# Value projections of four head pairs merged into two, in a two-layer FoX and retention trunk

## The chip, the core and the metric

The kernel runs on one core of one Trainium2 chip. The metric is the device time of one execution in microseconds (us), median of several runs. The kernel before takes 941.47 us (three runs, 941.02 to 941.47). The engines are named as in the profile: PE (TensorE, matmuls), PEld (its weight loads), DVE (VectorE), ACT (ScalarE), POOL (GpSimd), SP (SyncE, which here only issues DMAs).

## The reference

Two decoder layers over 512 positions of width 1024. Each makes one big input projection, attends in 12 main heads of 128 (layer 0: attention with a forget gate; layer 1: retention) and in 4 heads over a memory of 256 positions, multiplies by a SiLU gate, and projects out to the residual stream.

```python
for i in range(DEPTH):                       # 2
    h = rmsnorm(x, norm_g[i])
    proj = h @ (fox_w_in if i == 0 else ret_w_in)
    q, k, v, (f_logit,) q_mem, z = split_cols(proj, ...)
    main = fox_attention(q, k, v, f_logit, fox_b_f) if i == 0 else retention(q, k, v)
    memo = mem_cross_attention(q_mem, mem_n, w_mem_kv[i])
    o = concatenate([main, memo]) * silu(z)
    x = x + o @ w_out[i]
return rmsnorm(x, final_norm_g)
# in retention, q and k (64 wide a head) are rotated first:
#   concatenate([t1 * cos - t2 * sin, t1 * sin + t2 * cos])
```

Everything is float32. The kernel writes each operand as a high part H and a low part L in the fp32r type and makes every product of three matmuls (H·H, H·L, L·H).

## The kernel before, in words

**Matmuls.** Activations h lie transposed as hH and hL, 8 slices of 128 rows (`k`) by 512 positions. Weights come in 148 pieces of 128x1024 (`load_piece`, SP's queue, 3 `raw` buffers); `prep_piece` turns each into wH (a cast on ACT, L130) and wL (a subtraction on DVE, L131). There are 4 buffers of wH and of wL. When a piece's last matmul is written, `retire` frees it and at once writes the preparation of the next piece in the order of use.

**Fillers.** The dense work is cut into fillers, pieces of some 2.8 us of PE time. `f_T` (matmuls at L220) makes a projection with the weights stationary and the 512 positions moving: 24 matmuls in two fillers of 12. Through it go the gate `f_z`, the queries and keys of layer 0 and of the memory `f_q`, and the rotated queries and keys of layer 1 `f_rot`. `f_v` makes the value projection of a pair of heads the other way round: the positions of a block `t` of 128 are stationary, 256 weight columns move, so that one filler is 24 matmuls of 256 columns (`mm_group`, L60), and a pair takes 4 fillers. `f_out` (also L60) makes the output projection, 12 matmuls of 512 columns a block.

**Attention steps.** Between the fillers stand the steps of the attention of the current pair (`g_fox`, `g_ret`). In `g_ret` a step is a score (two matmuls, L60, of k and the two parts of q, into a tile `s`), the product with the values (`o`, two steps of six matmuls), and a norm (matmul of ones).

**The order.** PE is in the order in which the program writes it (`MANUAL`); the other engines are ordered by a scheduler, by a priority that each step gets from its filler's number. `build_layer` writes one `cycle` a pair: a list of fillers and the attention steps, spread over the fillers by `mode`. In cycle `pr` the attention of pair `pr` runs, and the fillers make the values of `pr`, the gates z0 and z1 of `pr`, and the queries and keys `nq` of pair `pr + 1`. The first score of a pair is written right behind the first filler of its cycle (the fifth for pair 0 of layer 1).

**The rotation.** In `f_rot` the finished projection (tile `acc`) is copied by ACT into `r` (L243), four DMAs on SP's queue swap its quarters into `sw` (L246), DVE multiplies and adds (L248, L249, L250), ACT casts (L254, L260), and DVE subtracts: L256 for k, L261 for q. The DVE work has the priority of four fillers later (`PRIO[3]`). Only behind the L256 of a head may a score read that head's k. In layer 1 the kernel before writes `nq` of pairs 1 and 3 ahead of z0 and z1, and `nq` of pairs 2 and 4 between the halves of the output projection, so that four fillers of its cycle come after the rotated k:

```python
            elif pr in (2, 4):
                o = f_out(l, (pr - 2, pr - 1))
                f = f + z0 + z1 + o[:4] + nq + o[4:]
...
            elif l == 0:
                f = f + z0 + z1 + nq
            else:
                f = f + nq + z0 + z1
```

**Tiles.** `vv` (5 buffers of 4 KB a partition) holds the values, the memory's values (in layer 1 reloaded by POOL, L441) and some row tiles; PSUM has 3 `acc`, 2 `s` and 3 tiles for transposes and `o`.

Of the kernel before, what the change touches and what calls it, by code (L numbers as in the profile page):

```python
# [9 lines left out]
F32R = mybir.dt.float32r  # L10
# [9 lines left out]
EPS = 1e-6  # L20
NEG_SCALE = -1.0 / math.sqrt(128.0)
BIG = 1e30
BUFS = dict(raw=3, w=4, qk=10, sqs=2, vv=5, gg=8, sz=2, pT=1, dd=5, p=2, cbc=2, km=6, acc=3, s=2, at=3)
TAGS = dict(acc="acc", s="s", t="at", o="at")
MANUAL = ("PE",)
TLS = False
# [10 lines left out]
def tile_hybrid(ctx, tc, x_in, mem_in, memT_in, g_cols, norm_g, fin_g, b_f, wv0, wp, index, consts, cosT, sinT, dec, out):  # L37
    nc = tc.nc
    P = 128
    KD = D // P  # L40
    NT = S // P
# [9 lines left out]
    def ps_at(kind, shape, dt, name):  # L51
        tag = TAGS[kind]
        return psum.tile(shape, dt, name=name, tag=tag, bufs=BUFS[tag])

    V, A, G, PE = nc.vector, nc.scalar, nc.gpsimd, nc.tensor
# [6 lines left out]
    def split3(lh, ll, rh, rl):  # L62
        return [(lh, rh), (lh, rl), (ll, rh)]
# [11 lines left out]
    def tile_(tag, shape, dt=F32):  # L75
        return work.tile(shape, dt, name=tag, bufs=BUFS[tag])

# [9 lines left out]
    hH = xp.tile([P, KD, S], F32R, name="hH")  # L87
    hL = xp.tile([P, KD, S], F32R, name="hL")
# [3 lines left out]
    st = {}  # L92
# [11 lines left out]
    raws, pieces = {}, {}  # L104
# [31 lines left out]
    def retire(*keys):  # L136
        for k in keys:
            pieces.pop(k)
            with due(first_use.get(order[min(nprep[0], len(order) - 1)], 0) + PRIO[2]):
                prep_piece()  # L140
# [8 lines left out]
    def split_to(dH, dL, src, scale=None):  # L149
        if scale is None:  # L150
            A.copy(out=dH, in_=src)  # L151
            V.tensor_tensor(out=dL, in0=src, in1=dH.bitcast(F32), op=ALU.subtract)
        else:
            A.activation(dH, src, AF.Copy, scale=scale)
            V.scalar_tensor_tensor(out=dL, in0=src, scalar=scale, in1=dH.bitcast(F32), op0=ALU.mult, op1=ALU.subtract)
# [6 lines left out]
    def acc_tile():  # L162
        return ps_at("acc", [P, 512], F32, name="acc")
# [102 lines left out]
    def f_v(l, pr):  # L266
        keys = [(l, "v", pr, i) for i in range(2)]
        first = l == 0 and pr == 0
        n = 268 if first else 256
        per = 1 if first else 2  # L270
        box = {}

        def part(t):
            if t == 0:
                st[l, "v", pr] = [tile_("vv", [P, 4, 256], F32R) for _ in range(2)]
                if first:
                    st["fl"] = small.tile([P, NT, 12], F32, name="fl", bufs=1)
            vH, vL = st[l, "v", pr]
            if t % per == 0:
                box["ps"] = acc_tile()  # L280
            ps, u = box["ps"], t % per
            terms = []
            for i, key in enumerate(keys):
                H, L = pieces[key]
                for k4 in range(4):
                    k = i * 4 + k4
                    terms += split3(hH[:, k, t * P:(t + 1) * P], hL[:, k, t * P:(t + 1) * P],
                                    H[:, k4 * n:(k4 + 1) * n], L[:, k4 * n:(k4 + 1) * n])
            mm_group(ps[:, u * 256:u * 256 + n], terms)
            if u == per - 1:  # L290
                src = ps[:, :per * 256].rearrange("p (u c) -> p u c", u=per)
                split_to(vH[:, t + 1 - per:t + 1, :], vL[:, t + 1 - per:t + 1, :], src)
                if first:
                    V.tensor_tensor(out=st["fl"][:, t, :], in0=ps[:, 256:268], in1=bfb, op=ALU.add)
            if t == NT - 1:
                retire(*keys)
        return [(keys if t == 0 else [], lambda t=t: part(t)) for t in range(NT)]

    def out_terms(l, pc, heads, t, c0=0, c1=512):
        H, L = pc  # L300
# [16 lines left out]
    def f_out(l, pairs):  # L317
        heads = [h for pr in pairs for h in (pr * 2, pr * 2 + 1)]
        res = []
        for hf in range(2):  # L320
            keys = [(l, "o", pr, hf) for pr in pairs]
            step = 3 - len(pairs)
            for t in range(0, NT, step):
                def fn(t=t, hf=hf, keys=keys):
                    for t2 in range(t, t + step):
                        out_block(l, [pieces[k] for k in keys], heads, t2, hf)
                    if t + step == NT:
                        retire(*keys)
                res.append((keys if t == 0 else [], fn))
        return res  # L330
# [385 lines left out]
    def build_layer(l):  # L716
        M = "fox" if l == 0 else "ret"
        fq = (lambda pr: f_q(0, "q", pr * 2, NEG_SCALE) + f_q(0, "k", pr * 2, None) +
              f_q(0, "q", pr * 2 + 1, NEG_SCALE) + f_q(0, "k", pr * 2 + 1, None)) if l == 0 else (
              lambda pr: f_rot(1, "q", pr) + f_rot(1, "k", pr))  # L720
        qm = [f_q(l, "qm", h, NEG_SCALE) for h in range(4)]
        cycle(f_v(l, 0) + qm[0] + qm[1], start=("lead", l))
        f0 = fq(0)
        cycle(f_z(l, 12) + f_z(l, 13) + qm[2] + qm[3] + (f0[:2] if l else []),
              attn_jobs("mem", l, (0, 1), 4) + ([] if l else [("forget", (), 0)]), start=("mem", l))
        cycle((f0[2:] if l else []) + f_z(l, 14) + f_z(l, 15) + ([] if l else f0), attn_jobs("mem", l, (2, 3), 4),
              mode=6 if l else None)
        for pr in range(6):
            f = [] if pr == 0 else f_v(l, pr)
            z0, z1 = f_z(l, pr * 2), f_z(l, pr * 2 + 1)  # L730
            nq = fq(pr + 1) if pr < 5 else []
            if pr == 0:
                f = f + z0 + z1 + nq + f_out(l, (6, 7))
            elif pr in (2, 4):
                o = f_out(l, (pr - 2, pr - 1))
                f = f + z0 + z1 + o[:4] + nq + o[4:]
            elif pr == 5:
                f = f + z0 + z1 + f_out(l, (4,))
            elif l == 0:
                f = f + z0 + z1 + nq  # L740
            else:
                f = f + nq + z0 + z1
            heads = (pr * 2, pr * 2 + 1)
            if l == 0:
                cycle(f, attn_jobs("fox", l, heads, 6), mode=SPAN5F if pr == 5 else None, last=pr == 5)
            else:
                base = 4 if pr == 0 else 0
                cycle(f, attn_jobs("ret2" if pr in (1, 3) else "ret", l, heads, 7, base),
                      mode=SPAN5 if pr == 5 else 14 + base, last=pr == 5)
# [9 lines left out]
          start="l1", mode=4)  # L759
# [113 lines left out]
def _vcols(w, cols, kper):  # L873
    import numpy as np
    a = np.concatenate([w[:, c0:c1] for c0, c1 in cols], axis=1)
    n = a.shape[1]
    a = a.reshape(8 // kper, kper, 128, n).transpose(0, 2, 1, 3)
    return [x.reshape(128, kper * n) for x in a]
# [79 lines left out]
```

## Time and profile before

| what | value |
|---|---|
| median of 3 runs | 941.47 us |
| the profiled execution's own time | 941.57 us |
| its span, first to last instruction | 939.8 us |
| PE busy | 924.9 us, 98% of the span, 5005 matmuls |
| PEld, DVE, ACT, POOL busy | 85%, 63%, 46%, 4% |
| mean granted TensorE clock | 0.995 of full |
| chain that ended last, PE's share | 95% |

The profile's page gives the busy share of each engine, the span in 40 slices with the granted clock, and the chain of work that ended last. Matmuls overlap in their pipeline, so the time of one instruction (about 390 ns with 512 columns) is longer than the distance to the next; what a filler costs is read from the chain in order of time or from the starts in the timeline. The timeline also gives, for a stretch, when each instruction began and what ended the engine's idle time before it.

### The profile page before, as it was taken

The numbers are of one execution on the slowest core, as the hardware profiler recorded it, in microseconds if no ns is written. First come the engines' busy times: TensorE is split into PE (matmuls) and PEld (weight loads), VectorE is DVE, ScalarE is ACT, GpSimd is POOL, SyncE is SP. The second block draws the span as 40 slices with busy tenths as digits, with TensorE's granted clock in tenths as the row PEclk, the third lists the DMA queues.
The fourth block names the chain that finished last, engine by engine and source line by source line (L and its number), as shares of the span: only waits on it lengthen the run. The fifth ranks groups of instructions, "written<-read, shape, count | busy, mean of one in ns | idle before, by whom it ended". The sixth has DMA issues, their size and how long they took to land.

```text
span 939.8 us, 13062 instructions
## 1 busy us (share of the span) xinstructions
PE 924.9 (98%) x5005; PEld 800.0 (85%) x5005; DVE 591.8 (63%) x1041; ACT 436.1 (46%) x747; POOL 34.1 (4%) x92
## 2 busy tenths in 40 slices
PE   8999999999999999999999999999999999999995
PEld 6988888889888889898898888888889888888984
DVE  5766564555645545655457856667767575856876
ACT  6654453433433324433334435546356454745564
POOL 0200100000000000000000100000000000000001
PEclk9999999999999999999999999999999999999998
DMA  8863332222323213222332152322342234333202
GB/s 290 334 216 111 109 108 89 82 86 79 114 68 102 93 59 118 84 96 68 103 101 90 45 177 71 90 90 79 101 132 74 93 107 122 103 101 105 89 21 90
DMA packets 32486, 100.74 MB, mean 107 GB/s; under 512 B 4380, under 2 KB 4636, under 8 KB 32424
## 3 DMA queue, kind: packets, MB, share of 16 engines
q1 hardware_dynamic: 30840, 96.76, 31.7%
q0 software_dynamic: 864, 2.10, 0.7%
q10 hardware_dynamic: 720, 1.05, 0.3%
q8 instruction: 39, 0.64, 0.3%
q14 instruction: 23, 0.19, 0.1%
HBM read 92.53 MB, written 4.22 MB: 103 GB/s over the span
## 4 chain that ended last, share of the span: by engine, by line
PE 95%; ACT 1%; DVE 1%; POOL 1%; issue 1%; DMA 0%; POOLq 0%; ACTq 0%; DVEq 0%
PE acc L220 44%; PE acc L60 32%; PE s L60 6%; PE o L512 5%; PE acc L408 3%; PE pt L546 1%; PE o L60 1%; PE pt L481 1%; PE acc L353 1%; PE acc L347 1%; PE pt L196 1%; ACT dd L772 0%; DMA vv<-in_memT_dram 0%; DVE wL L131 0%; POOL rstd L188 0%
## 5 line engine op out<-in xcount | busy, mean ns | idle before, releaser
L131 DVE TENSOR_TENSOR wL<-raw,wH 128x1024 fp32r<-128x1024 f32 x148 | 180.9, 1223 | 133.3 <-ACT wH L130 75.6
L130 ACT CAST wH<-raw 128x1024 fp32r<-128x1024 f32 x148 | 154.8, 1051 | 100.3 <-PE acc L220 53.7
L220 PE MATMUL acc<-hL,wH 128*128 128x512 f32 x608 | 162.8, 394 | 0.0
L220 PE MATMUL acc<-hH,wH 128*128 128x512 f32 x608 | 153.5, 394 | 0.0
L220 PE MATMUL acc<-hH,wL 128*128 128x512 f32 x608 | 150.6, 390 | 0.0
L60 PE MATMUL acc<-wH,gg 128*128 128x512 f32 x448 | 146.1, 393 | 0.0
L220 PEld LDWEIGHTS acc<-hH,wL 128*128 128x128 f32 x608 | 114.1, 188 | 24.4
L220 PEld LDWEIGHTS acc<-hH,wH 128*128 128x128 f32 x608 | 111.1, 188 | 21.2
L220 PEld LDWEIGHTS acc<-hL,wH 128*128 128x128 f32 x608 | 111.3, 188 | 20.7
L60 PE MATMUL acc<-wH,hH 128*128 128x256 f32 (+1 forms) x384 | 109.4, 285 | 0.0
L60 PE MATMUL acc<-wH,hL 128*128 128x256 f32 (+1 forms) x384 | 108.7, 283 | 0.0
L60 PE MATMUL acc<-wL,hH 128*128 128x256 f32 (+1 forms) x384 | 108.6, 283 | 0.0
L60 PEld LDWEIGHTS acc<-wH,gg 128*128 128x128 f32 x448 | 84.2, 188 | 17.0
L60 PE MATMUL acc<-wL,gg 128*128 128x512 f32 x224 | 87.3, 390 | 0.0
L310 DVE TENSOR_TENSOR x<-acc,x 128x512 f32<-128x512 f32 x80 | 54.8, 688 | 40.6 <-PE acc L60 38.5
L60 PEld LDWEIGHTS acc<-wL,hH 128*128 128x128 f32 x384 | 73.4, 191 | 0.4
L60 PEld LDWEIGHTS acc<-wH,hH 128*128 128x128 f32 x384 | 73.3, 191 | 0.5
L60 PEld LDWEIGHTS acc<-wH,hL 128*128 128x128 f32 x384 | 73.3, 191 | 0.0
L536 ACT ACTIVATE p<-dd,nm 128x128 f32<-128x128 f32 (+3 forms) x48 | 27.0, 563 | 66.3 <-DVE nm L532 66.1
L151 ACT CAST pTH<-pt 128x128 fp32r<-128x128 f32 (+2 forms) x64 | 29.7, 467 | 56.6 <-PE pt L546 43.9
L60 PE MATMUL s<-qk 128*128 128x256 f32 (+3 forms) x240 | 54.5, 328 | 0.6 <-DVE p L586 0.6
L151 ACT CAST gg<-sz 128x512 fp32r<-128x512 f32 x32 | 19.9, 621 | 74.7 <-DVE sz L447 31.5
(154 smaller groups left out, 1187.2 us busy)
## 6 DMA issues: line engine op xcount, KB each, us to landing
raw<-in_wp_dram SPq DMA_DIRECT2D x146, 512.0 KB, 3.5
cbc<-c_d SPq DMA_DIRECT2D x12, 256.0 KB, 3.3
cbc<-in_dec_dram SPq DMA_DIRECT2D x12, 256.0 KB, 3.7
dd<-dd SPq DMA_DIRECT2D x48, 64.0 KB, 2.0
x<-in_x_dram SPq DMA_DIRECT2D x4, 512.0 KB, 7.7
raw<-in_wv_dram SPq DMA_DIRECT2D x2, 536.0 KB, 4.1
vv<-in_memT_dram SPq DMA_DIRECT2D x2, 512.0 KB, 4.5
vv<-in_mem_dram SPq DMA_DIRECT2D x2, 512.0 KB, 7.7
```

Source lines behind the costliest of these rows:

```text
L60: PE.matmul(ps, lhsT=l, rhs=r, start=(i == 0), stop=(i == n - 1))
L130: A.copy(out=H[:, :n], in_=raw[:, :n])
L131: V.tensor_tensor(out=L[:, :n], in0=raw[:, :n], in1=H[:, :n].bitcast(F32), op=ALU.subtract)
L151: A.copy(out=dH, in_=src)
L196: PE.transpose(pt[:, k, :], xn[:, c:c + P], ident)
L220: PE.matmul(box["ps"], lhsT=a[:, k * P:(k + 1) * P], rhs=b[:, k, :], start=(n == 0), stop=(n == 23))
L310: V.tensor_tensor(out=dst, in0=ps, in1=dst, op=ALU.add)
L347: PE.matmul(ps, lhsT=a, rhs=b, start=(i == 0), stop=False)
L353: PE.matmul(ps, lhsT=a, rhs=b, start=False, stop=(i == 2))
L408: PE.matmul(box[b], lhsT=a, rhs=w, start=(i == 0 and n == 0), stop=(i == 3 and n == 5))
L512: PE.matmul(o[:, j * P:], lhsT=a, rhs=b, start=(j == 0 and i == 0), stop=(j == NT - 1 and i == 2))
L536: A.activation(p[:, :n], dd[:, :n], AF.Exp, bias=nm, scale=-1.0, accum_out=sm)
```

## The change

The values of pairs 1 and 2, and of pairs 3 and 4, are made together by a new function `f_v2`: for each block `t` of 128 positions 24 matmuls with 512 moving columns, in two fillers (`hf`) of 12. Its weights are four pieces of two `k` slices with 512 columns, in place of two pieces a pair of four slices with 256 columns; the number of pieces and of bytes stays. The first four of the eight fillers (blocks 0 and 1) stand at the end of the cycle before, the other four at the start of cycles 1 and 3. Cycles 2 and 4 have no value projection of their own. Each block's result is split into the two pairs' tiles with two casts and two subtractions of 256 columns. `vv` gets two more buffers, and the scratch for POOL's DMA descriptors is set to 8192 bytes a partition.

The order of fillers in the cycles changes too: in cycle 0 the last two fillers of `nq` come behind the output projection; in cycles 2 and 4 `nq` but for its last two fillers comes ahead of the output projection and these two behind it; and in cycles 1 and 3 of layer 1 `nq` now comes behind z0 and z1, as in layer 0.

```diff
-BUFS = dict(raw=3, w=4, qk=10, sqs=2, vv=5, gg=8, ...
+BUFS = dict(raw=3, w=4, qk=10, sqs=2, vv=7, gg=8, ...
...
+    def f_v2(l, prs):
+        keys = [(l, "v2", prs[0], i) for i in range(4)]
+        box = {}
+
+        def part(t, hf):
+            if (t, hf) == (0, 0):
+                for pr in prs:
+                    st[l, "v", pr] = [tile_("vv", [P, 4, 256], F32R) for _ in range(2)]
+            if hf == 0:
+                box["ps"] = acc_tile()
+            ps = box["ps"]
+            ts = slice(t * P, (t + 1) * P)
+            for i in (2 * hf, 2 * hf + 1):
+                H, L = pieces[keys[i]]
+                for k2 in range(2):
+                    k, c = 2 * i + k2, slice(k2 * 512, (k2 + 1) * 512)
+                    for n, (a, b) in enumerate(split3(hH[:, k, ts], hL[:, k, ts], H[:, c], L[:, c])):
+                        PE.matmul(ps, lhsT=a, rhs=b, start=(k == 0 and n == 0), stop=(k == KD - 1 and n == 2))
+                if t == NT - 1:
+                    retire(keys[i])
+            if hf:
+                for u, pr in enumerate(prs):
+                    vH, vL = st[l, "v", pr]
+                    split_to(vH[:, t, :], vL[:, t, :], ps[:, u * 256:(u + 1) * 256])
+        return [(keys[2 * hf:2 * hf + 2] if t == 0 else [], lambda t=t, hf=hf: part(t, hf)) for t in range(NT) for hf in range(2)]
...
+        v2 = {pr: f_v2(l, (pr, pr + 1)) for pr in (1, 3)}
         for pr in range(6):
-            f = [] if pr == 0 else f_v(l, pr)
+            f = v2[pr][4:] if pr in v2 else []
...
             if pr == 0:
-                f = f + z0 + z1 + nq + f_out(l, (6, 7))
+                f = f + z0 + z1 + nq[:-2] + f_out(l, (6, 7)) + nq[-2:] + v2[1][:4]
             elif pr in (2, 4):
                 o = f_out(l, (pr - 2, pr - 1))
-                f = f + z0 + z1 + o[:4] + nq + o[4:]
+                f = f + z0 + z1 + nq[:-2] + o + nq[-2:] + (v2[3][:4] if pr == 2 else [])
             elif pr == 5:
-                f = f + z0 + z1 + f_out(l, (4,))
-            elif l == 0:
+                f = f_v(l, 5) + z0 + z1 + f_out(l, (4,))
+            else:
                 f = f + z0 + z1 + nq
-            else:
-                f = f + nq + z0 + z1
...
-    nc = bacc.Bacc("TRN2", target_bir_lowering=False, num_devices=1)
+    nc = bacc.Bacc("TRN2", target_bir_lowering=False, num_devices=1, dynamic_dma_scratch_size=8192)
```

Three places show how the order moves. Lines of the changed program are 26 higher from `f_v2` on (score L612, `o` L538, gate L638), names end in the number of the buffer.

First, PE where the values of pair 1 begin in layer 0. Before, a block of pair 1 alone, followed by the first score of that pair:

```order
L60 MATMUL acc_2162<-wH_2068,hH_86 128x256
L60 MATMUL acc_2162<-wL_2069,hH_86 128x256
L60 MATMUL acc_2162<-wH_2068,hL_87 128x256
L60 MATMUL s_2194<-qk_1814,qk_1766 128x128
L60 MATMUL s_2194<-qk_1815,qk_1766 128x128
L60 MATMUL s_2194<-qk_1814,qk_1767 128x128
```

Now, a block of pairs 1 and 2 behind the last key projection of cycle 0, before that cycle ends:

```order
L220 MATMUL acc_2107<-hL_87,wH_2014 128x512 x4
L220 MATMUL acc_2107<-hH_86,wL_2015 128x512 x8
L316 MATMUL acc_2164<-wH_2020,hH_86 128x512
L316 MATMUL acc_2164<-wL_2021,hH_86 128x512
L316 MATMUL acc_2164<-wH_2020,hL_87 128x512
```

The three products of a slice `k` now move 512 columns each, for two pairs at a time.

Second, PE from the rotated k of pair 2 on, at the border of cycles 1 and 2 of layer 1. Before, `acc_6686` is this k's projection, `acc_6767` and `acc_6808` are the gates of pair 1, the `s` are scores of head 3; behind these rows stand the rest of `acc_6808`, six matmuls of `o` and 24 of `f_v` ahead of the first score that reads the new k (`s_6898`):

```order
L220 MATMUL acc_6686<-hL_87,wH_6433 128x512 x4
L220 MATMUL acc_6686<-hH_86,wL_6434 128x512 x8
L60 MATMUL s_6760<-qk_6157,qk_6221 128x256
L60 MATMUL s_6760<-qk_6159,qk_6221 128x256
L220 MATMUL acc_6767<-hH_86,wH_6602 128x512 x8
L220 MATMUL acc_6767<-hL_87,wH_6602 128x512 x4
L60 MATMUL s_6780<-qk_6157,qk_6221 128x128
L60 MATMUL s_6780<-qk_6159,qk_6221 128x128
L220 MATMUL acc_6767<-hL_87,wH_6602 128x512 x4
L220 MATMUL acc_6767<-hH_86,wL_6603 128x512 x8
L220 MATMUL acc_6808<-hH_86,wH_6608 128x512 x8
L220 MATMUL acc_6808<-hL_87,wH_6608 128x512 x4
```

Now, `acc_6647` is this k's projection, `acc_6719` the first gate of pair 2, and `s_6736` the first score of head 4, which reads the rotated k `qk_6695`:

```order
L220 MATMUL acc_6647<-hL_87,wH_6456 128x512 x4
L220 MATMUL acc_6647<-hH_86,wL_6457 128x512 x8
L538 MATMUL o_6666<-pTH_6534,vv_6256 128x256
L538 MATMUL o_6666<-pTL_6535,vv_6256 128x256
L538 MATMUL o_6666<-pTH_6534,vv_6257 128x256
L538 MATMUL o_6666<-pTH_6534,vv_6256 128x128
L538 MATMUL o_6666<-pTL_6535,vv_6256 128x128
L538 MATMUL o_6666<-pTH_6534,vv_6257 128x128
L220 MATMUL acc_6719<-hH_86,wH_6501 128x512 x8
L220 MATMUL acc_6719<-hL_87,wH_6501 128x512 x4
L60 MATMUL s_6736<-qk_6629,qk_6695 128x512
L60 MATMUL s_6736<-qk_6631,qk_6695 128x512
```

Between this k and its first reader there were four fillers of 12, a filler of `f_v` and some attention; now there is one filler of 12 and half a step of `o`. The border of cycles 3 and 4 is the same, and at that of cycles 4 and 5 there stands one filler of `f_v` (24 matmuls of 256 columns) alone.

Third, DVE at the same border. Before, from the last add of this k's rotation (`dd_6738`) to the product of the first score `s_6898` with its decay table:

```order
L250 TENSOR_TENSOR dd_6738<-dd_6738,dd_6739 128x512
L236 SCALAR_TENSOR_TENSOR sz_6799<-sz_6799,acc_6767 128x512
L256 TENSOR_TENSOR qk_6748<-dd_6738,qk_6748 64x512
L612 SCALAR_TENSOR_TENSOR sz_6799<-o_6627,sz_6799 128x512
L256 TENSOR_TENSOR qk_6751<-dd_6738,qk_6751 64x512
L613 TENSOR_TENSOR sz_6799<-sz_6799,dd_6713 128x512
L131 TENSOR_TENSOR wL_6803<-raw_6612,wH_6802 128x1024
L152 TENSOR_TENSOR gg_6824<-sz_6799,gg_6823 128x512
L131 TENSOR_TENSOR wL_6850<-raw_6672,wH_6849 128x1024
L236 SCALAR_TENSOR_TENSOR sz_6846<-sz_6846,acc_6808 128x512
L152 TENSOR_TENSOR sqs_6864<-p_6861,sqs_6863 128x512
L612 SCALAR_TENSOR_TENSOR sz_6846<-o_6827,sz_6846 128x512
```

Now, from the piece that the last matmul of `acc_6647` frees (`wL_6702`) to the product of the first score `s_6736`; `dd_6685` and `dd_6686` are this k's, `dd_6619` is q's:

```order
L131 TENSOR_TENSOR wL_6702<-raw_6505,wH_6701 128x1024
L250 TENSOR_TENSOR dd_6619<-dd_6619,dd_6620 128x512
L638 SCALAR_TENSOR_TENSOR sz_6571<-o_6666,sz_6571 128x512
L152 TENSOR_TENSOR sqs_6716<-p_6713,sqs_6715 128x512
L261 TENSOR_TENSOR qk_6631<-dd_6619,qk_6629 64x512
L261 TENSOR_TENSOR qk_6637<-dd_6619,qk_6635 64x512
L248 TENSOR_TENSOR dd_6686<-dd_6686,km_5068 128x512
L249 TENSOR_TENSOR dd_6685<-dd_6685,km_5066 128x512
L250 TENSOR_TENSOR dd_6685<-dd_6685,dd_6686 128x512
L256 TENSOR_TENSOR qk_6695<-dd_6685,qk_6695 64x512
L256 TENSOR_TENSOR qk_6698<-dd_6685,qk_6698 64x512
L612 TENSOR_TENSOR p_6739<-s_6736,cbc_6732 128x512
```

Before, nine other instructions stood between the first L256 and that product; now only the second L256 does, and six stand between the last matmul of the projection and the rotation's L248.

## Rows read from the trace of the kernel before

**Rows 1.** The page, busy time by engine, and the granted clock in 40 slices.

```profile
PE 924.9 (98%) x5005; PEld 800.0 (85%) x5005; DVE 591.8 (63%) x1041; ACT 436.1 (46%) x747; POOL 34.1 (4%) x92
...
PEclk9999999999999999999999999999999999999998
```

**Rows 2.** The page, chain that ended last, shares of the span by engine.

```profile
PE 95%; ACT 1%; DVE 1%; POOL 1%; issue 1%; DMA 0%; POOLq 0%; ACTq 0%; DVEq 0%
```

**Rows 3.** That chain in order of time, layer 0, cycle 1: start us, us, what.

```profile
222.32 2.92 PE acc L60 x24
...
225.60 2.88 PE acc L60 x24
...
232.91 2.75 PE acc L220 x12
```

**Rows 4.** Timeline, layer 1, rotation of pair 5's k: start us, us, engine, line, instruction.

```profile
862.52 1.98 PE L220 MATMUL acc<-hH,wL 128*128 128x512 f32 x8
...
864.33 0.39 PE L60 MATMUL acc<-wH,gg 128*128 128x512 f32 x1
...
864.53 0.59 ACT L243 COPY dd<-acc 128x512 f32<-128x512 f32 x1 [0.76 <-PE acc L220]
...
865.15 2.41 SPq L246 DMA_DIRECT2D dd<-dd  x4
...
869.59 0.69 DVE L248 TENSOR_TENSOR dd<-dd,km 128x512 f32<-128x512 f32 x1
...
870.20 0.69 DVE L249 TENSOR_TENSOR dd<-dd,km 128x512 f32<-128x512 f32 x1
...
871.82 0.68 DVE L250 TENSOR_TENSOR dd<-dd 128x512 f32<-128x512 f32 x1
...
872.54 1.26 ACT L254 CAST qk<-dd 64x512 fp32r<-64x512 f32 x2 [1.91 <-DVE dd L250]
...
873.19 1.40 DVE L256 TENSOR_TENSOR qk<-dd,qk 64x512 fp32r<-64x512 f32 x2 [0.69 <-ACT qk L254]
...
873.73 0.28 PE L512 MATMUL o<-pTH,vv 128*128 128x256 f32 x1
...
874.37 0.44 PE L60 MATMUL acc<-wH,gg 128*128 128x512 f32 x1
...
880.06 0.40 PE L60 MATMUL s<-qk 128*128 128x512 f32 x1
```

**Rows 5.** Timeline, the same steps for pair 1's k.

```profile
641.59 0.59 ACT L243 COPY dd<-acc 128x512 f32<-128x512 f32 x1 [0.76 <-PE acc L220]
...
642.21 2.41 SPq L246 DMA_DIRECT2D dd<-dd  x4
...
646.35 0.69 DVE L248 TENSOR_TENSOR dd<-dd,km 128x512 f32<-128x512 f32 x1
```

**Rows 6.** Groups of DVE: line, engine, operation, count, busy us, mean ns, idle before.

```profile
L131 DVE TENSOR_TENSOR wL<-raw,wH 128x1024 fp32r<-128x1024 f32 x146 | 178.3, 1223 | 132.8 <-ACT wH L130 75.2 <-PE acc L220 54.1 <-PE pt L546 2.1
...
L612 DVE SCALAR_TENSOR_TENSOR sz<-o,sz 128x512 f32<-128x512 f32 x12 | 8.3, 689 | 2.3 <-ACT p L599 2.2
...
L152 DVE TENSOR_TENSOR vv<-acc,vv 128x256 fp32r<-128x256 f32 x4 | 1.7, 422 | 4.7 <-ACT vv L151 4.7
```

**Rows 7.** Stretches: sum, busy us (instructions) by engine, granted clock, DMA share, GB/s.

```profile
7.20:9.00 1.80, 0.55 (x2) 0.24 (x2) 1.35 (x3) 1.80 (x4) 0.00 (x0) 1.00 1.01 401
9.00:12.40 3.40, 3.40 (x8) 2.75 (x9) 3.40 (x6) 3.40 (x7) 0.00 (x0) 0.50 1.03 410
930.50:934.00 3.50, 0.00 (x0) 0.00 (x0) 3.27 (x6) 1.97 (x6) 1.05 (x3) 1.00 0.61 235
934.00:939.80 5.80, 0.00 (x0) 0.00 (x0) 0.77 (x2) 1.04 (x3) 0.81 (x2) 0.50 0.34 130
```

**Rows 8.** Timeline, layer 1: POOL's second load of memory values, and their first reader.

```profile
541.80 0.54 POOL L441 DMA_DIRECT2D vv<-vmd  x1 [1.05 <-DVE vv L189]
...
576.36 0.39 PE L60 MATMUL o<-pTH,vv 128*128 128x512 f32 x1
```

More of the change, by code (lines that the diff above doesn't have):

```diff
@@ L22 @@
 BIG = 1e30
-BUFS = dict(raw=3, w=4, qk=10, sqs=2, vv=5, gg=8, sz=2, pT=1, dd=5, p=2, cbc=2, km=6, acc=3, s=2, at=3)
+BUFS = dict(raw=3, w=4, qk=10, sqs=2, vv=7, gg=8, sz=2, pT=1, dd=5, p=2, cbc=2, km=6, acc=3, s=2, at=3)
 TAGS = dict(acc="acc", s="s", t="at", o="at")
@@ L918 @@
                 continue
-            for i, a in enumerate(_vcols(w, [(v0 + pr * 256, v0 + pr * 256 + 256)], 4)):
-                add(a, l, "v", pr, i)
+            if pr in (1, 3):
+                for i, a in enumerate(_vcols(w, [(v0 + pr * 256, v0 + pr * 256 + 512)], 2)):
+                    add(a, l, "v2", pr, i)
+            elif pr in (0, 5):
+                for i, a in enumerate(_vcols(w, [(v0 + pr * 256, v0 + pr * 256 + 256)], 4)):
+                    add(a, l, "v", pr, i)
         for pr in range(8):
```

## The prediction

> **What bounds the kernel now.** I read the page first: PE is busy 98% of the span, DVE 63%, ACT 46%, and the granted clock is full in every slice but the last [rows 1]. The chain that ended last lies on PE for 95% [rows 2]. So the kernel is a stream of matmuls, and a change moves the time in two ways only: by what PE's stream costs, and by what PE has to wait for. Then I read that chain in order of time for the price of a filler [rows 3], and the timeline for one step that the change moves, the rotation of k in layer 1: how long it takes from its last matmul to its first reader [rows 4, 5]. The groups give the price of single instructions [rows 6], two stretches at each end what the clock does when matmuls pause [rows 7].
>
> **Merged matmuls: a gain of 4.2 us.** An `f_v` filler of 24 matmuls with 256 columns took 2.92 and 2.88 us, an `f_T` filler of 12 with 512 took 2.75 [rows 3]. Both move the same number of columns, so what differs is a price for each matmul. Four pairs in two layers have 4 fillers each: 32 fillers of the first kind become 32 of the second. 32 x (2.88 - 2.75) = 4.2 us, all on PE's path. From below I bound it by nothing (the difference may lie in where these fillers stand), from above by the other row: 32 x 0.17 = 5.4 us. I take 4.2, since 2.88 is the filler that stands among its like.
>
> The Trainium skill, page "TensorE: Matmul & The Clock Gate", section "Back-to-back issue gap", gives the distance of two warm matmuls as the columns at 2.4 GHz plus 2.5 ns; by that the merge would save an estimated 384 x 2.5 ns = 1.0 us, and the sum below would be 3.2 us higher. The rows speak for some five times as much, so the term goes by them.
>
> **What the merge asks for beside PE.** Eight evictions of 256 columns replace four of 512 in each merge. On DVE that is 8 x 0.42 for 4 x 0.69 us [rows 6], 0.6 us more, and ACT has about as much; each engine idles over a third of the span [rows 1], and three `acc` tiles lie between them and PE. If that cover were gone, it would cost 4 x 0.6 us. The merge holds all four weight buffers, but the next filler's piece is freed 18 matmuls before it is needed, 4.1 us at the price of an `f_T` filler [rows 3], and its first 12 matmuls read only the cast part; the subtraction of 1.22 us [rows 6] has 2.75 us more. The last of the four pieces is freed when the filler ahead ends and read 18 matmuls into the merge, again 4.1 us. Each costs nothing while these 4.1 us hold. The number of pieces, bytes and SP issues stays. The smaller descriptor scratch touches only POOL's reloads of memory operands: the second load was issued at 541.8, its first reader came at 576.4 [rows 8]. A delay under the 34 us between costs nothing.
>
> **The moved rotations: three waits, 15.5 us.** This is the term that decides. In layer 1 the rotated k of pairs 2, 4 and 5 is now the last projection of its cycle, and the first score of the next cycle reads it one filler later. How long is it from the last matmul of that projection (T) to the finished k?
>
> In the rows for pair 5 the last matmul ends at 862.52 + 1.98 = 864.50, the copy at 865.12; four swaps follow on SP's queue, 2.41 us for issuing them alone [rows 4]. For pair 1 the copy ended at 642.18 and the first multiplication began at 646.35, 4.2 us later [rows 5]. So the multiplication starts at T + 0.6 + 4.2 = T + 4.8. On DVE the new order puts six instructions ahead of it: a weight subtraction of 1.22 and five of about 0.69 us [rows 6], 4.7 us, so the queue is done by then as well. From there: 0.61 to the second multiplication and its 0.69, then the add; 0.72 from the add to the cast; 0.65 to the subtraction; 0.70 for the first of two [rows 4]. That is 3.4 us, and k is ready at T + 8.2. In the kernel before, these steps took from 864.50 to 873.89 and nobody waited: the score came at 880.06 [rows 4].
>
> PE reaches the score much earlier now. Its next matmul starts 0.17 us before T; half a step of `o` takes 0.64 [rows 4], the gate's filler 2.75 [rows 3]: T + 3.2. It waits 8.2 - 3.2 = 5.0 us, at the borders of cycles 1 and 2 and of cycles 3 and 4. At the border of cycles 4 and 5 only an `f_v` filler of 2.88 stands between, so T + 2.7 and a wait of 5.5 us; there DVE has only the weight subtraction ahead, and the swaps alone set 4.8. Sum: 5.0 + 5.0 + 5.5 = 15.5 us. PE's order is fixed, so everything behind the score waits with it, and as PE is the bound, nothing later gives it back. The swaps also stand in SP's queue ahead of one weight load; that load is for a piece used three preparations later.
>
> Bounds: the multiplication can't start before the fourth swap is issued, at T + 0.6 + 2.4. That gives k at T + 6.4 and waits of 3.2, 3.2 and 3.7, 10.1 us. From above I take the whole of the rows for pair 5, 9.4 us from T to k, in which another add had slipped in: 6.2, 6.2 and 6.7, 19.1 us. I take 15.5, the sum of steps as the order now has them.
>
> The rotations that stay covered: pairs 1 and 3, whose k has four merged fillers and one more behind it, over 13 us, and all of layer 0, where keys are only split.
>
> **The clock after these waits: 4.7 us.** With no matmul after 930.5 the granted clock stayed full for 3.5 us and was half, 1.2 GHz in place of 2.4, from 934.0 on; early on it was half from 9.0 to 12.4, right after a stretch of 1.8 us in which PE had only two matmuls [rows 7]. A wait of 5 us is longer than either. The half stretch held 8 matmuls in 3.4 us [rows 7], where a filler's price makes it 8 x 0.229 = 1.8 us [rows 3]: 1.6 us lost. I take one such stretch a wait, 3 x 1.57 = 4.7 us; bounds none and two a wait, 9.4.
>
> The Trainium skill says on the same page, section "HAM oscillation — how this bites in real kernels", that waits between bursts put PE back to the slow clock and each burst then starts cold; the end of this trace agrees, the middle of it has no such wait to show it.
>
> **Sum.** The profiled execution took 941.6 us, 0.1 above the median. 941.6 - 4.2 + 15.5 + 4.7 = 957.6; against the median **957.5 us**, slower by 1.7%.
>
> **Rivals.**
> 1. *The waits come, the clock holds.* For it: the clock was full in all stretches between, with PE's short waits. Against: both ends of the trace. 957.5 - 4.7 = 952.8 us.
> 2. *The merge saves nothing*, the difference of the fillers being one of place. For it: the rows are of different lines. Against: both kinds stand among the same attention steps. 957.5 + 4.2 = 961.7 us. The skill's rule on the issue gap, cited above, would lie close to this one.
> 3. *The rotation hides, and the kernel is faster.* Mechanism: with PE standing or ahead, DVE, ACT and SP are free, and the chain shrinks to what PE still has to do. Place: the three borders. Price: nothing left of 15.5 and 4.7, 941.5 - 4.2 = 937.3 us. It decides from the point where the three waits together stay under 4.2 us, that is 1.4 each or k at T + 4.6. Against: the multiplication alone began at T + 4.8 in rows where it waited for swaps, and 3.4 us of dependent steps follow. For: only that the swaps' landing was seen in a few rows.
> 4. *The clock costs two stretches a wait.* 957.5 + 4.7 = 962.2 us.
> That the change doesn't do what it says is ruled out by the order: the merged matmuls and the moved k stand there.
>
> **How the numbers follow.** Forecast 0.72, rival 1 0.15, rival 2 0.05, rival 3 0.04, rival 4 0.04. A measurement of this kernel can tell about 0.2%, 1.9 us, from no change. Faster by more: rival 3 but for its partial cases, 0.03; no change 0.01; slower 0.96. The range goes from rival 1 with half the way to its lower bound of waits, 952.8 - 2.6 = 950.2, to the forecast with waits at their upper bound, 957.5 + 3.6, and half of a second clock stretch, + 2.3: 963.4. It leaves out rival 3 and the ends of the others, under 2 in 10.
>
> **What would show it.** Right: PE has 384 matmuls fewer; the chain's merged fillers (L316) take 2.75 us; among PE's waits stand three of about 5 us for a score, released by DVE's `qk` of L256, in layer 1 alone; behind each the granted clock falls to half for a few us. The step on the rotation is wrong if PE waits there under 2 us, that on the clock if it stays full across the waits, that on the merge if an L316 filler takes 2.88. The whole is wrong if the time is below 946: then something hides the rotations that I have put at 8.2 us, or the merge gives far more than its rows say.

## The result, and the profile after

| | before | after |
|---|---|---|
| median of 4 runs each, side by side | 941.47 us (941.02 to 941.64) | 956.0 us (955.12 to 958.31) |
| ratio | | 1.0159, 95% interval [1.0146, 1.0172] |
| the profiled execution, its span | 941.57 us, 939.8 us | 956.54 us, 954.8 us |

The kernel is slower by 1.6%; the forecast was 957.5 us. The page of the changed kernel, for [rows 1, 2]: busy times, granted clock in 40 slices, and the chain that ended last by engine.

```profile
PE 926.0 (97%) x4621; PEld 783.3 (82%) x4621; DVE 592.5 (62%) x1057; ACT 441.9 (46%) x767; POOL 34.5 (4%) x92
...
PEclk9999999999999999999999999999999999999998
...
PE 93%; ACT 2%; DVE 2%; DMA 1%; POOL 1%; issue 0%; SPq 0%; POOLq 0%; DVEq 0%; ACTq 0%
```

PE has 384 matmuls fewer, as said. The slices, 24 us each, are too coarse for what happened to the clock. PE's waits, with the total, the count and the longest (us), show what is new:

```profile
PE s L60 <- DVE qk L256: 14.4, 3, 5.1
PE acc L434 <- DVE wL L131: 1.6, 2, 0.9
```

Three waits of a score for the rotated k, 14.4 us together, which the kernel before did not have; the next in size are 1.6 us. No wait of PE stands at a merged filler or an eviction, and none in layer 0 is of this kind. The merged fillers in the chain in order of time (start, us, what), for [rows 3]:

```profile
219.73 13.60 PE acc L316 x60
...
233.61 2.79 PE acc L316 x12
...
236.75 2.75 PE acc L316 x12
```

Five in a row take 13.60 / 5 = 2.72 us each, single ones 2.75 to 2.79, where the fillers of 24 took 2.88 and 2.92. Now the border of cycles 1 and 2 in the timeline of the changed kernel, for [rows 4, 5]:

```profile
716.76 1.53 PE L220 MATMUL acc<-hH,wL 128*128 128x512 f32 x6
...
718.32 0.59 ACT L243 COPY dd<-acc 128x512 f32<-128x512 f32 x1 [0.77 <-PE acc L220]
...
718.76 2.06 PE L220 MATMUL acc<-hH,wH 128*128 128x512 f32 x8
...
718.94 2.41 SPq L246 DMA_DIRECT2D dd<-dd  x4
...
720.66 1.08 PE L220 MATMUL acc<-hL,wH 128*128 128x512 f32 x4
...
722.17 0.69 DVE L261 TENSOR_TENSOR qk<-dd,qk 64x512 fp32r<-64x512 f32 x1 [0.17 <-ACT qk L254]
...
723.01 0.69 DVE L248 TENSOR_TENSOR dd<-dd,km 128x512 f32<-128x512 f32 x1
723.62 0.68 DVE L249 TENSOR_TENSOR dd<-dd,km 128x512 f32<-128x512 f32 x1
724.33 0.69 DVE L250 TENSOR_TENSOR dd<-dd 128x512 f32<-128x512 f32 x1
...
725.71 1.40 DVE L256 TENSOR_TENSOR qk<-dd,qk 64x512 fp32r<-64x512 f32 x2 [0.68 <-ACT qk L254]
...
726.45 1.22 PE L60 MATMUL s<-qk 128*128 128x512 f32 x2 [4.71 <-DVE qk L256]
```

The last matmul of the projection ends at T = 716.76 + 1.53 = 718.29; the score starts at T + 8.16, after 4.71 us in which PE did nothing. The multiplication L248 begins 0.15 us after DVE's queue ahead of it is done (722.17 + 0.69 = 722.86), and 0.19 us after the last of the four swaps landed (722.82, in the trace's record of landings), so the two ended together. At the border of cycles 3 and 4 the wait is 4.64. At that of cycles 4 and 5 DVE was free, and L248 waited for the swaps:

```profile
886.22 2.41 SPq L246 DMA_DIRECT2D dd<-dd  x4
...
890.08 0.69 DVE L248 TENSOR_TENSOR dd<-dd,km 128x512 f32<-128x512 f32 x1 [3.19 <-DMA dd<-dd]
...
893.53 1.22 PE L60 MATMUL s<-qk 128*128 128x512 f32 x2 [5.08 <-DVE qk L256]
```

The clock, read by stretches (columns as in [rows 7]: PE's and PEld's busy us first, then the other engines; the granted clock follows POOL):

```profile
12.70:726.00 713.30, 707.81 (x3618) 601.86 (x3616) 435.26 (x812) 314.48 (x570) 29.49 (x74) 1.00 0.34 109
726.02:729.43 3.41, 2.98 (x7) 2.40 (x8) 2.10 (x4) 1.27 (x3) 0.00 (x0) 0.50 0.00 0
...
835.25:838.66 3.41, 3.19 (x8) 2.51 (x9) 2.10 (x4) 1.27 (x3) 0.00 (x0) 0.50 0.00 0
893.27:896.69 3.42, 3.16 (x12) 2.97 (x13) 2.62 (x5) 1.16 (x3) 0.00 (x0) 0.50 0.00 1
```

From 12.7 us on the clock is full up to the first of these waits; at the end of each wait it falls to half, 1.2 GHz, for 3.4 us. In these stretches PE was busy for 2.98 + 3.19 + 3.16 = 9.3 us, and at full clock the same matmuls would take half: 4.7 us lost, by this estimate.

### The profile page after: what moved, and what is told of

It reads as the page before. It is cut to its first block, busy times and chain, and to the rows that moved or that the text cites. A ratio compares the mean times of both kernels' runs of the same rounds, so it can differ in the third digit from the quotient of the medians.

```text
span 954.8 us, 12306 instructions
## 1 busy us (share of the span) xinstructions
PE 926.0 (97%) x4621; PEld 783.3 (82%) x4621; DVE 592.5 (62%) x1057; ACT 441.9 (46%) x767; POOL 34.5 (4%) x92
## 4 chain that ended last, share of the span: by engine, by line
PE 93%; ACT 2%; DVE 2%; DMA 1%; POOL 1%; issue 0%; SPq 0%; POOLq 0%; DVEq 0%; ACTq 0%
PE acc L220 43%; PE acc L60 22%; PE acc L316 9%; PE s L60 6%; PE o L538 5%; PE acc L434 3%; PE pt L572 1%; PE o L60 1%; PE pt L507 1%; PE acc L379 1%; PE acc L373 1%; PE pt L196 1%; DMA dd<-dd 0%; ACT dd L797 0%; DMA vv<-in_memT_dram 0%
## 5 line engine op out<-in xcount | busy, mean ns | idle before, releaser
L60 PE MATMUL s<-qk 128*128 128x256 f32 (+3 forms) x240 | 56.4, 336 | 14.9 <-DVE qk L256 14.4
L60 PEld LDWEIGHTS s<-qk 128*128 128x128 f32 x240 | 41.0, 193 | 22.7 <-DVE qk L256 15.5
L316 PE MATMUL acc<-wH,hH 128*128 128x512 f32 x128 | 50.4, 394 | 0.0
L316 PE MATMUL acc<-wH,hL 128*128 128x512 f32 x128 | 49.9, 390 | 0.0
L316 PE MATMUL acc<-wL,hH 128*128 128x512 f32 x128 | 49.9, 389 | 0.0
L60 PEld LDWEIGHTS acc<-wL,gg 128*128 128x128 f32 x224 | 42.2, 188 | 7.8
L538 PE MATMUL o<-pTH,vv 128*128 128x512 f32 (+1 forms) x192 | 48.4, 314 | 0.0
L152 DVE TENSOR_TENSOR pTL<-pt,pTH 128x128 fp32r<-128x128 f32 (+2 forms) x64 | 34.2, 536 | 22.1 <-ACT pTH L151 21.9
```

Source lines behind the costliest of these rows:

```text
L60: PE.matmul(ps, lhsT=l, rhs=r, start=(i == 0), stop=(i == n - 1))
L316: PE.matmul(ps, lhsT=a, rhs=b, start=(k == 0 and n == 0), stop=(k == KD - 1 and n == 2))
L538: PE.matmul(o[:, j * P:], lhsT=a, rhs=b, start=(j == 0 and i == 0), stop=(j == NT - 1 and i == 2))
```

## The experiments

The theory: the merge gains 4 to 5 us; the moved rotation makes three waits; each wait brings the clock down for a while. The rivals are those of the prediction. Kernel medians are compared with the kernel before, run on the same chip beside them (941.23, 940.97 and 941.63 us in the three series).

### The merge alone, the order alone

The changed kernel with layer 1's rotated keys put back ahead of other fillers:

```diff
             elif pr in (2, 4):
                 o = f_out(l, (pr - 2, pr - 1))
-                f = f + z0 + z1 + nq[:-2] + o + nq[-2:] + (v2[3][:4] if pr == 2 else [])
+                if l == 1 and pr == 4:
+                    f = f + z0 + z1 + nq + o
+                else:
+                    f = f + z0 + z1 + nq[:-2] + o + nq[-2:] + (v2[3][:4] if pr == 2 else [])
...
-            else:
+            elif l == 0:
                 f = f + z0 + z1 + nq
+            else:
+                f = f + nq + z0 + z1
```

> The merged values stay; in layer 1 the rotated queries and keys go back ahead of the gates in cycles 1 and 3, and in cycle 4 ahead of the whole output projection, so that every rotated k has at least four fillers behind it. Theory (the loss is three waits for rotated keys and the slow clock behind them, the merge itself gains 4.2 us): no wait of PE over 1 us in layer 1, the clock full throughout, 941.5 - 4.2 = 937.3 us, between 936 and 938.5. Rival (the merge, with four weight pieces held and smaller evictions, gains nothing or costs): 941.5 us or more.

Measured: 936.57 us (935.51 to 936.64), ratio 0.9946 [0.9934, 0.9959]. None of the three waits is left; of PE's waits for a tile `s` the profile names

```profile
PE s L60 <- DVE p L612: 0.6, 2, 0.3
```

and from 12.4 to 930.4 us the granted clock is 1.00. The merge gains 941.23 - 936.57 = 4.7 us, and this version beats both kernels. It also keeps the buffers and the new order of cycles 0 and 2, so the 4.7 us are those of the merge together with these.

The kernel before with the changed order in layer 1 only, nothing merged:

```diff
             elif pr in (2, 4):
                 o = f_out(l, (pr - 2, pr - 1))
-                f = f + z0 + z1 + o[:4] + nq + o[4:]
+                if l == 1 and pr == 4:
+                    f = f + z0 + z1 + nq[:-2] + o + nq[-2:]
+                else:
+                    f = f + z0 + z1 + o[:4] + nq + o[4:]
...
-            elif l == 0:
-                f = f + z0 + z1 + nq
             else:
-                f = f + nq + z0 + z1
+                f = f + z0 + z1 + nq
```

> The kernel before, value projections unmerged, with the changed place of the rotated queries and keys of layer 1 alone (behind the gates in cycles 1 and 3, last in cycle 4). Theory: the same three waits of 4.6 to 5.1 us for the subtraction at L256 and three half-clock stretches, 941.5 + 14.4 + 4.7 = 960.6 us, between 959 and 962. Rival (the waits need the merge too, since it holds the weight buffers and adds evictions): clearly under 955 us.

Measured: 962.13 us (961.79 to 963.16), ratio 1.0224 [1.0208, 1.024], with

```profile
PE s L60 <- DVE qk L256: 14.1, 3, 5.1
```

The three waits come from the order and not from the merge. The time lies 0.1 us above the expected range, because of the clock: it fell behind each wait here too, for 3.4, 6.8 and 6.8 us, in which PE was busy for 13.2 us: 6.6 us lost, 1.9 more than in the changed kernel. The missing merge and this make 4.7 + 1.9 = 6.6 us; the two medians are 6.1 apart.

### The clock: waits filled, and half filled

The changed kernel with matmuls that nobody reads, ahead of the first score at each of the three borders (20, later 10):

```diff
+            if l == 1 and pr in (2, 4, 5):
+                def padded(fn=f[0][1]):
+                    fn()
+                    pad = acc_tile()
+                    for i in range(PAD):
+                        PE.matmul(pad, lhsT=hH[:, 0, 0:P], rhs=hH[:, 1, :], start=(i == 0), stop=(i == PAD - 1))
+                f = [(f[0][0], padded)] + f[1:]
```

> The changed kernel with 20 matmuls of 512 columns, whose result nobody reads, ahead of the first score at the three borders where PE waits (4.6 us of work in a wait of 4.6 to 5.1). Theory: PE's matmuls run on, the clock stays full, the rotated key comes at the same time, and the time falls by the clock's share alone: 956.0 - 4.7 = 951.3 us, between 950.3 and 952.3. Rival (the half-clock stretches cost nothing, since PE catches up or was not bound there): 956 us. If the added work delayed anything, over 956.

Measured: 953.86 us (953.32 to 954.36), ratio 1.0133 [1.0119, 1.0147]. The stretch from 7.2 us on and PE's waits (lines are one higher here):

```profile
7.20:946.70 939.50, 928.56 (x4668) 785.97 (x4668) 591.15 (x1054) 439.39 (x763) 33.37 (x86) 1.00 0.32 105
```

```profile
PE s L61 <- DVE qk L257: 2.8, 3, 1.4
```

The clock part holds: it stayed full to the end. The size was missed (951.3 was expected), since k came later than in the changed kernel at two borders of three: 20 matmuls fill 4.6 us, and 0.16, 1.40 and 1.21 us of waiting stood on top. At the two late borders the swaps landed 2.7 and 3.4 us after their issue (median of four) in place of 2.0, and one packet of the instruction queue (q8) ran among them, which the changed kernel has there at neither. From 827.9 to 832 us, DMA queues and issues with their landing:

```profile
q1 hardware_dynamic: 207, 0.58, 47.1%
q8 instruction: 1, 0.02, 2.0%
...
dd<-dd SPq DMA_DIRECT2D x1, 64.0 KB, 3.4
```

Whether that packet is the cause wasn't tried. It is not enough by itself: in the order-alone version such a packet ran from 820.03 to 821.48, and the swaps issued from 820.81 on landed after 2.0 us all the same.

> The changed kernel with ten unread matmuls (in place of the twenty of the earlier run) ahead of the first score at each of the three borders: they fill 2.3 us of each wait of 4.6 to 5.1, and 2.3 to 2.8 us of PE's pause stay. Theory that k's readiness is fixed by ACT, SP and DVE, and the clock's fall by the length of PE's pause: the waits shrink to 2.3 to 2.8 us, the score starts when it did; if a pause of that length doesn't bring the clock down, 956.0 - 4.7 = 951.3 us (950.3 to 952.5) with the clock full from the start to the end, and if it does, 956.0 (954.5 to 957.5) with a half-clock stretch behind each border. With twenty the time was 953.9 and k was ready later than in the changed kernel; should the added matmuls themselves have delayed the swaps, this run lies between 951.3 and 953.9.

Measured: 954.74 us (953.62 to 956.44), ratio 1.0146 [1.0133, 1.016]. The waits were 2.42, 2.33 and 2.79 us: with the 2.3 us of added matmuls 4.7, 4.6 and 5.1, just as in the changed kernel. So ten added matmuls do not delay k; ACT, DVE and the swaps set it. On the clock the run stands between its two cases:

```profile
7.30:833.20 825.90, 818.33 (x4122) 693.60 (x4122) 513.35 (x931) 380.02 (x670) 29.36 (x74) 1.00 0.32 109
833.31:836.72 3.41, 3.41 (x10) 2.63 (x9) 1.98 (x3) 3.00 (x5) 0.00 (x0) 0.50 0.02 5
...
891.34:894.75 3.41, 3.41 (x16) 3.31 (x16) 2.52 (x5) 1.03 (x2) 0.00 (x0) 0.50 0.02 5
```

The clock held across the first wait (2.42 us), and fell behind the second (2.33) and the third (2.79). The length of a wait alone does not decide at this size.

### One border put back

The changed kernel with only the first hunk of the merge-alone version, so that the rotated k of pair 5 has the output projection behind it.

> The changed kernel with only cycle 4 of layer 1 set right: rotated queries and keys ahead of the whole output projection. Theory: one wait of 5.1 us and one slow stretch of 1.6 us fewer, two of each left: 956.0 - 6.7 = 949.3 us, between 948 and 950.5. Rival (what is saved at one border is lost at a later one, for instance at the last output projections): 953 us or more.

Measured: 950.55 us (949.65 to 950.78), ratio 1.0096 [1.0083, 1.011], 5.5 us below the changed kernel and just above the expected range. PE's waits, and the stretches at half clock:

```profile
PE s L60 <- DVE qk L256: 9.3, 2, 4.7
```

```profile
723.92:730.75 6.83, 5.60 (x13) 4.44 (x14) 2.76 (x4) 4.66 (x7) 0.00 (x0) 0.50 0.00 0
833.15:839.97 6.82, 4.66 (x11) 3.69 (x12) 3.46 (x6) 3.88 (x6) 0.00 (x0) 0.50 0.03 11
```

The one wait of 5.1 us is gone, the other two are as they were (4.71 and 4.59). But each was now followed by 6.8 us at half clock, where the same waits in the changed kernel had 3.4. The waits are fixed; the price of the clock behind them is not.

### The buffers alone

The kernel before with `vv=7` and `dynamic_dma_scratch_size=8192`, nothing else.

> The kernel before with seven value buffers in place of five and the smaller descriptor scratch, and nothing else of the change. The forecast put both at nothing: 941.5 us (940.8 to 942.2), a ratio within 0.1% of 1. Rival: the smaller scratch makes POOL's reloads late, or the two buffers move the order of DVE and ACT so that PE waits; then the time is over 943 us and PE's waits show a new releaser.

Measured: 940.98 us (940.7 to 941.97, 11 runs) beside 940.97 (15 runs), ratio 1.0001 [0.9992, 1.0009]. Nothing, as said.

### What sets when k is ready

The changed kernel with the four swap DMAs on two queues:

```diff
-                nc.sync.dma_start(out=sw[b * 32:(b + 1) * 32, :], in_=r[s0:s0 + 32, :])
+                (nc.sync if b % 2 == 0 else nc.scalar).dma_start(out=sw[b * 32:(b + 1) * 32, :], in_=r[s0:s0 + 32, :])
```

> The changed kernel, with two of the four swap DMAs of each rotation issued on ACT's queue and two on SP's, so that the last is issued 1.2 us earlier. Theory: at the border of cycles 4 and 5 the swaps alone set when k is ready, so the wait there (5.1 us) falls by about 1.2 us; at the other two borders DVE has six instructions (4.7 us) ahead of the multiplication, done at about the same time as the swaps, so their waits (4.7 and 4.6) fall by 0 to 0.5 us. With two to three half-clock stretches left, 954.6 us (952 to 957). Rival: the swaps' issue is not what sets the start, their landing is, with the same delay after the first one however they are issued; then all three waits stay at 4.6 to 5.1 and the time at 956. Second rival: with the issue halved, everything on the chain comes 1.2 us earlier at all three borders; then three waits of 3.4 to 3.9 us and about 952.4 us.

Measured: 960.32 us (960.03 to 962.18), ratio 1.0203 [1.0187, 1.0219]: slower than the changed kernel, and outside what the theory and both rivals gave. At the border of cycles 4 and 5 the wait fell by 0.85 us, to 4.23; at the other two it grew to 6.55 and 6.51. The timeline of the first:

```profile
718.85 1.14 SPq L246 DMA_DIRECT2D dd<-dd  x2
718.86 0.52 ACTq L246 DMA_DIRECT2D dd<-dd  x1
...
720.09 0.54 SPq L118 DMA_DIRECT2D raw<-in_wp_dram  x1
...
720.13 0.52 ACTq L246 DMA_DIRECT2D dd<-dd  x1
...
724.35 0.69 DVE L248 TENSOR_TENSOR dd<-dd,km 128x512 f32<-128x512 f32 x1 [2.16 <-DMA dd<-dd]
```

ACT had a cast and an activation between its two swaps, so that SP, done early with its own, issued the weight load ahead of the last swap. From 720.1 us on, the issues with the time to landing:

```profile
raw<-in_wp_dram SPq DMA_DIRECT2D x1, 512.0 KB, 3.9
dd<-dd ACTq DMA_DIRECT2D x1, 64.0 KB, 4.0
```

That swap took 4.0 us to land, with a load of 512 KB in flight beside it, where the changed kernel's four, ahead of the load on one queue, took 2.0. The Trainium skill, page "DMA: Bandwidth & Descriptors", section "Queues, rings and completion order", says that each DMA engine takes turns between the queues it has work for, and drains a whole packet of descriptors from one before it switches. The trace fits turns as long as the load's share of an engine: from 721.0 to 722.75 us only SP's queue moved data, the swap's first transfer began at 722.81, and it landed 0.1 us after the load issued just ahead of it (720.13 + 4.0, 720.09 + 3.9). That this share is one such packet isn't shown; the packets that the profile counts are single transfers of 2 or 4 KB. To tell this from a slow ACT queue, only the first swap went to ACT, right behind the copy:

```diff
-                nc.sync.dma_start(out=sw[b * 32:(b + 1) * 32, :], in_=r[s0:s0 + 32, :])
+                (nc.scalar if b == 0 else nc.sync).dma_start(out=sw[b * 32:(b + 1) * 32, :], in_=r[s0:s0 + 32, :])
```

> The changed kernel with only the first of the four swap DMAs on ACT's queue, directly behind the copy that it reads, and the other three on SP's, still ahead of the weight load. In the run with two and two the second of ACT's swaps was issued 1.9 us after the copy at the first two borders, because ACT had other work in between; by then SP had issued the 512 KB weight load, and that swap landed 4.0 us after its issue, where the changed kernel's took 2.0. Theory (the swaps' issue counts, and a weight load issued ahead of a swap delays its landing): here no load is ahead of any swap and the last swap is issued 0.6 us earlier than in the changed kernel, so the wait at the border of cycles 4 and 5 falls from 5.1 to about 4.5 us, and the other two stay within 4.2 to 4.7, since DVE's instructions ahead end then; with one to two half-clock stretches a border, 955.5 us (953.5 to 958.5). Rival (ACT's queue itself is slow for these swaps, whatever stands in between): the swap on ACT's queue lands late here too, and all three waits are 5.5 us or more, 958.5 to 962 us.

Measured: 957.03 us (956.61 to 957.62), ratio 1.0166 [1.0149, 1.0183]. ACT's swap landed after 2.2 to 2.3 us at all three borders: the queue is not slow by itself. The wait at the border of cycles 4 and 5 is 4.45, 0.6 us shorter, as expected from the swaps' issue. The other two were expected at 4.2 to 4.7 and are 5.12 us. The timeline of the first:

```profile
717.56 0.59 ACT L243 COPY dd<-acc 128x512 f32<-128x512 f32 x1 [0.77 <-PE acc L220]
...
720.67 0.69 DVE L152 TENSOR_TENSOR sqs<-p,sqs 128x512 fp32r<-128x512 f32 x1 [0.60 <-ACT sqs L151]
...
721.93 0.69 DVE L261 TENSOR_TENSOR qk<-dd,qk 64x512 fp32r<-64x512 f32 x1 [0.57 <-ACT qk L254]
722.65 0.69 DVE L248 TENSOR_TENSOR dd<-dd,km 128x512 f32<-128x512 f32 x1
...
726.10 1.22 PE L60 MATMUL s<-qk 128*128 128x512 f32 x2 [5.12 <-DVE qk L256]
```

L248 starts as the last L261 ends, without waiting for a swap, but 5.09 us after the copy in place of 4.69: ACT's order had shifted, and DVE waited 0.60 and 0.57 us for it ahead of L248. So in this version DVE's queue sets the start at these two borders (the last swap had landed 1.2 us earlier, at 721.42), and the swaps at the third. In the changed kernel the two ended within 0.04 us of each other at the first two borders.

### The sum over all runs

Do the three terms account for every kernel? From 941.2 us, the median of the kernel before in the first series: less 4.7 where merged (this figure is the merge-alone run's own), plus the waits, the added matmuls at 0.229 us, and half of PE's busy time at half clock, against the profiled execution. Waits and clock are read from each run's own trace.

| kernel | merge | waits | added | clock | sum | profiled |
|---|---|---|---|---|---|---|
| changed | -4.7 | 14.4 | | 4.7 | 955.6 | 956.5 |
| order alone | | 14.1 | | 6.6 | 961.9 | 962.1 |
| waits filled | -4.7 | 2.8 | 13.7 | 0 | 953.0 | 953.3 |
| half filled | -4.7 | 7.5 | 6.9 | 3.4 | 954.3 | 954.0 |
| one border back | -4.7 | 9.3 | | 5.1 | 950.9 | 950.4 |
| two queues | -4.7 | 17.3 | | 8.3 | 962.1 | 962.2 |
| one swap on ACT | -4.7 | 14.7 | | 6.0 | 957.2 | 957.3 |

They agree within 0.9 us. Left out is the half-clock stretch at 9 us of [rows 7], which stood in some profiles and not in others, the changed kernel's among those with it. It costs some 0.9 us: the kernel before has it and a span of 939.8 us, the version with the buffers alone has not and a span of 938.9, and PE is apart by about as much from 21 us on.

## Why the prediction was right

**Merge: -4.2 forecast, -4.7 measured.** Right in kind, 0.5 us too small. The 32 merged fillers take 87.8 us in the chain, 2.745 each, so that the chain shows 32 x (2.88 - 2.745) = 4.3; the other 0.4 is no more than the spread of single runs (941.02 to 941.64) and isn't placed. The rival by which the merge saves nothing is out. So are the 1.0 us that went with it: the run shows 4.7 us / 384 = 12 ns for each matmul saved in this data type, in place of 2.5. The Trainium skill's page "TensorE: Matmul & The Clock Gate", section "Back-to-back issue gap", gives the 2.5 ns for an isolated matmul, and says itself that in a stream of weight loads and matmuls both set the spacing; the prediction used it for such a stream.

**Evictions, pieces, scratch and buffers: nothing forecast, nothing found.** No PE wait stands there, and the buffers alone gave 1.0001.

**Waits: 15.5 forecast, 14.4 measured.** All three stood where the order put them, in layer 1 alone. The chain from the projection to k was put at 8.2 us and took 8.16. Most of the difference is one of counting: the profile counts PE's idle time from the end of the last matmul, which in a full stream overlaps the next. From starts, the filler that begins at 718.76 would let the score begin 2.75 us later, at 721.51, T + 3.2 as forecast; the stream loses 726.45 - 721.51 = 4.94 us there, 4.86 at the second border in the same way, and 5.08 + 0.16 = 5.24 at the third (0.28 us for a matmul of 256 columns that ends the stretch, 0.12 for one within it), 15.0 in all. At the last border the swaps let L248 start at T + 4.5 (T = 885.57), not T + 4.8. The 4.8 was misread: the prediction took the 4.2 us between copy and multiplication in [rows 5] for the swaps' time, but there DVE was busy until 646.31, and the last swap had landed at 646.08, 4.5 us after the projection. The kernel before, ahead of that L248:

```profile
644.92 1.39 DVE L261 TENSOR_TENSOR qk<-dd,qk 64x512 fp32r<-64x512 f32 x2
```

That DVE's six instructions and the swaps end at about the same time at the first two borders was said, and they do, within 0.04 us; which of the two decides can't be told there. At the third it is the swaps alone. The rival that hides the rotation would have needed waits under 1.4 us each; the shortest was 4.64.

**Clock: 4.7 forecast, 4.7 in the profiled execution.** The mechanism is shown: with the waits filled the clock stayed full. The rival in which it holds across the waits (952.8 us) is out. The size was in part luck. The same waits were followed by 3.4 us at half clock in one profile and by 6.8 in others, so that the rival with two stretches a wait was right for one border back and for two waits of three in three more versions (order alone, two queues, one swap on ACT). The changed kernel's own runs spread over 3.2 us, from 955.12 to 958.31, with a mean granted clock of 0.991 and 0.986, the kernel before's over 0.6; the term's bounds, none to two stretches, were the right thing to keep in the range. The Trainium skill's section "HAM oscillation — how this bites in real kernels" on the same page, "TensorE: Matmul & The Clock Gate", has the clock go slow after each wait between bursts; behind every one of the 14 waits of 4.2 us or more, in the profiles of five versions, the trace agrees, and behind the three of 2.3 to 2.8 us it fell twice.

Not placed: the 0.9 us between the sum and the changed kernel's profiled time. The waits counted by starts would give 0.6 of it, and the stretch at 9 us, which only some runs of the kernel before contain, up to 0.4. But the same two corrections would put the version with two queues some 0.9 us too high, so the account doesn't hold to better than that.

## What to carry to other kernels

When a change reorders independent work on the engine that bounds the kernel, ask of each moved producer how long its chain on the other engines is, and what work now stands between it and its first reader: here 8.2 us of copy, swaps and small vector instructions against 3.4 us of matmuls. A saving of 4.7 us in matmul count was lost four times over (14.4 + 4.7 = 19.1 us) in an order that had nothing to do with it, and the merge with the old order in layer 1 keeps the saving (936.57 us). A pause of the matmul stream is to be priced with the clock that it can bring down behind it, and as a range.

## What the runs showed of the hardware that was not expected

- Behind waits of the same length in the same place (4.71 us at the border of cycles 1 and 2) the clock was at half for 3.4 us in the changed kernel and for 6.8 with one border put back. With two queues it was at half for 6.8 us behind a wait of 6.55, and for 10.2 behind one of 6.51. A wait of 2.42 us left it full where one of 2.33 did not. What decides between them stays open.

```profile
726.11:732.93 6.82, 5.14 (x12) 4.08 (x13) 3.02 (x5) 4.35 (x6) 0.00 (x0) 0.50 0.00 0
835.33:845.57 10.24, 5.91 (x14) 4.66 (x15) 4.74 (x7) 5.13 (x7) 0.00 (x0) 0.50 0.00 0
```

- Four swap DMAs of 64 KB in a row on one queue landed 2.0 us after their issue; one issued on the other queue 0.04 us behind a load of 512 KB took 4.0 us. Spreading the four over two queues made the last of them later at two borders of three, since it let a large one in ahead.
